# A hybrid decoder trunk: TensorE's instruction order written out for the scan layer, in five bunches a group, and for the last attention head

## The chip, the cores and the metric

One core of one Trainium2 chip runs the whole program once. The metric is device time in microseconds (us), the median of the runs taken. The engines are named as in the profile: PE is TensorE's matmuls and PEld its weight loads, DVE is VectorE, ACT is ScalarE, POOL is GpSimd, SP is the engine that issues most DMAs.

## The reference

The model has four residual layers over a sequence of 512 tokens of width 1024: dilated attention, a gated convolution FFN, a Mamba-2 mixer, and a second FFN, and then a final norm. The change touches the end of the attention, all of the Mamba-2 mixer and the start of the FFN behind it. Shortened:

```python
def ssd_mixer(h, ...):                       # h = rmsnorm(x)
    zxbcdt = h @ w_in                        # 1024 -> z 2048, xs 2048, B 1024, C 1024, dt 32
    xbc = silu(causal_depthwise_conv(xbc, conv_w, conv_b))      # 4 taps
    xs, bm, cm = ...                         # 32 heads of 64; 8 groups of B and C, 128 states
    dt = softplus(dt_raw + dt_bias); a = -exp(a_log)
    y = ssd_chunked_scan(xs, dt, a, bm, cm)  # 4 chunks of 128 tokens:
        # y_diag = ((C B^T) * lmat) (xs dt),  lmat[i,j] = exp(min(cs_i - cs_j, 0)), j <= i
        # states = B^T (decay xs dt), carried over the chunks; y_off = C states * exp(cs)
    y = gated_group_rmsnorm(y + d_skip * xs, z, norm_w, SSM_GROUPS)  # y*silu(z), rms over 256
    return y @ w_out                         # 2048 -> 1024

x = x + dilated_attention_mixer(rmsnorm(x), ...)   # 8 heads, 3 dilations, softmax over the three
x = x + conv_ffn(rmsnorm(x), ...)                  # (silu(gate) * up) @ w_down
x = x + ssd_mixer(rmsnorm(x), ...)
x = x + conv_ffn(rmsnorm(x), ...)
return rmsnorm(x)
```

## The kernel before, in words

Activations lie feature by token, 128 features by 512 tokens in a tile. Each float32 product is made of three float32r products (`mm3`, L129): high part times high part, high times low, low times high. A tile of 128 outputs over 1024 inputs is therefore 24 matmuls of 128x512. The weights are fetched by `load_unit` (L109): a DMA on SP into `raw` (3 buffers), the high part by a cast on ACT (`hi`), the low part by a subtraction on DVE or, for the gate `z`, on POOL (`lo`). `hi` and `lo` have 4 buffers each.

The scan layer works on 8 groups. `project_group` (L639) makes the six products of a group: two of xs, b, c, two of z; on each follow a scaling from PSUM by DVE (`us`, L630), a 4-tap convolution (ACT L510 and three DVE steps L512) and a silu on ACT. `decay_rates` (L576), once at the start, turns the product `wdt` into step sizes by some twenty small DVE steps (`dtw`, then `adt`), sums them by PE (`pa`, `prow`), and writes them to memory as `rows`, from which each head's decay tile `lm` is read back. `scan_group` (L654) is a generator with six steps between its yields: (1) transposes `px`, `pb` and the product `pc`, which make `xdt`, `btok` and `cb`; (2) the decay tiles of two heads, the states `pst`, a second `px`; (3) the outputs `py`, `pf` of the first half, decays and states of the second; (4) the outputs of the second half and `gsq`, the sum of both halves' squares (L762); (5) `ss`, the sum over features by PE, and `rg` on POOL; (6) `prg`, the spreading of `rg` by PE, and the scaled `y`. `write_groups` (L777) makes the output products `wso` from finished `y`, 12 matmuls for two groups.

`weave` runs a generator's steps and puts a share of a list of other work (`fill`) behind each: for group g the six products of group g+1 and the output products of groups long finished. What order the instructions then take on each engine is settled by the tile framework's own scheduler, which may move any instruction past another, except where `tc.manual_schedule` names engines: there these engines keep the order in which the code is written. Before, that holds for PE in `outputs`, in the later part of `last_group`, and at the starts of the FFNs. Once built, the order is fixed: every engine works its list from the front and waits at the first instruction whose inputs are late.

In the attention, head h is worked (`attend`, L347) beside the projections of head h+1: three pairs `qk` (scaled by DVE, rotated by POOL, L321 to L326) and `v`, turned by PE (`pv`). Head 7 has no next head; beside it stand its own `v` and the first parts of the output products `wo` (`wo_first`, L466), which need heads 0 to 6 only; the last head's part (`o7h`, `o7l`) is added at L501.

## Time and profile before

| | us |
|---|---|
| median of 3 runs (1676.91 to 1684.19) | 1677.9 |
| the profiled execution, whole | 1678.81 |
| its span, first to last instruction | 1677.0 |
| PE busy in the span | 1654.9 |
| DVE busy | 1075.1 |
| ACT busy | 693.2 |
| POOL busy | 469.9 |
| PE idle before `wo`, waiting for ACT's `o7h` | 2.1 |
| PE idle before `pf`, waiting for DVE's `prev` | 2.1 |

PE is busy 99% of the span, so all the time in which it does nothing is 22.1 us. The other engines' idle time matters only where PE waits for them. In the rows below, a time in front is that from the span's start; "[2.10 <-ACT o7h L449]" is idle time of the engine and what ended it. Matmuls overlap: a 128x512 product takes 0.38 us from its start to its end, but the next one starts some 0.22 us after it. On DVE, too, one instruction starts a little (some 0.08 us) ahead of the end of the one in front.

### The profile page before, as it was taken

The page shows a single profiled execution, that of the slowest core. Times are in us where ns is not written, and L with a number is a line of the kernel's source. Part 1 is how long each engine was busy: PE and PEld are TensorE (multiplying, and loading weights), DVE is VectorE, ACT ScalarE, POOL GpSimd, SP SyncE. Part 2 cuts the span into 40 slices and gives each one's busy share as a digit, 9 for nine tenths or more (in the row PEclk, how much of TensorE's full clock was granted, in tenths as well). Part 3 has the DMA queues.
Part 4 walks back from the last instruction along what each step waited for, and adds up shares of the span by engine and source line. Part 5 has one row for each costly group of instructions (what it writes and reads, how often), then busy time and mean ns, then how long its engine had stood idle before and what let it go on. Part 6 is the DMA issues. An engine that isn't in the chain of part 4 may idle for free. (4 is left out here: it accounts for less than half of the span.)

```text
span 1677.0 us, 21515 instructions
## 1 busy us (share of the span) xinstructions
PE 1654.9 (99%) x8224; PEld 1401.9 (84%) x8224; DVE 1075.1 (64%) x1794; ACT 693.2 (41%) x1020; POOL 469.9 (28%) x305
## 2 busy tenths in 40 slices
PE   9999999999999999999999999999999999999997
PEld 8888888888888888888888788888888888888887
DVE  5466564366656745745657888787787684574564
ACT  5223332333244423423445665555562542342345
POOL 0443443144413211211232223233222331121124
PEclk9999999999999999999999999999999999999999
DMA  6321222222223323323233222332321232322324
GB/s 218 108 88 64 89 76 88 95 82 76 78 99 126 98 85 107 101 89 113 79 100 132 95 94 95 94 101 101 113 95 56 97 113 88 103 98 89 113 79 135
DMA packets 52343, 165.56 MB, mean 99 GB/s; under 512 B 5841, under 2 KB 8145, under 8 KB 52241
## 3 DMA queue, kind: packets, MB, share of 16 engines
q1 hardware_dynamic: 51152, 163.15, 29.2%
q8 instruction: 65, 1.06, 0.3%
q10 hardware_dynamic: 1088, 1.05, 0.2%
q14 instruction: 38, 0.30, 0.1%
HBM read 162.01 MB, written 2.16 MB: 98 GB/s over the span
## 5 line engine op out<-in xcount | busy, mean ns | idle before, releaser
L127 PE MATMUL u<-xl,hi_u 128*128 128x512 f32 x704 | 270.0, 384 | 1.8 <-DVE xl L176 1.8
L127 PE MATMUL u<-xh,hi_u 128*128 128x512 f32 x704 | 270.3, 384 | 0.0
L127 PE MATMUL u<-xh,lo_u 128*128 128x512 f32 x704 | 269.9, 383 | 0.0
L532 POOL TENSOR_TENSOR au<-au,au 128x512 f32<-128x512 f32 x44 | 57.9, 1316 | 431.9 <-DVE au L512 411.2
L512 DVE SCALAR_TENSOR_TENSOR au<-usu,par,au 128x510 f32<-128x510 f32 (+1 forms) x176 | 162.2, 926 | 6.6 <-ACT au L510 1.7
L325 POOL TENSOR_TENSOR rotqk<-rotqk,sr 32x512 f32<-32x512 f32 x48 | 91.9, 1914 | 257.4 <-DVE rotqk L324 210.0
L118 ACT CAST hi_u<-raw_u 128x1024 fp32r<-128x1024 f32 x88 | 91.1, 1042 | 156.6 <-PE u L127 102.9
L127 PEld LDWEIGHTS u<-xl,hi_u 128*128 128x128 f32 x704 | 131.9, 187 | 27.2 <-DVE xl L176 2.2
L127 PEld LDWEIGHTS u<-xh,lo_u 128*128 128x128 f32 x704 | 131.9, 187 | 25.2
L127 PEld LDWEIGHTS u<-xh,hi_u 128*128 128x128 f32 x704 | 131.9, 187 | 25.2
L127 PE MATMUL qk<-xh,hi_qk 128*128 128x512 f32 x384 | 149.1, 388 | 0.0
L127 PE MATMUL qk<-xl,hi_qk 128*128 128x512 f32 x384 | 148.2, 386 | 0.0
L127 PE MATMUL qk<-xh,lo_qk 128*128 128x512 f32 x384 | 147.1, 383 | 0.0
L527 DVE TENSOR_TENSOR usu<-u,rbc 128x512 f32<-128x512 f32 x88 | 60.5, 690 | 110.6 <-PE u L127 101.3
L119 DVE TENSOR_TENSOR lo_u<-raw_u,hi_u 128x1024 fp32r<-128x1024 f32 x88 | 109.7, 1251 | 24.7 <-ACT hi_u L118 24.7
L545 DVE TENSOR_TENSOR xr<-xr,wd 128x512 f32<-128x512 f32 x40 | 27.2, 686 | 117.1 <-PE wd L127 117.1
L118 ACT CAST hi_qk<-raw_qk 128x1024 fp32r<-128x1024 f32 x48 | 50.2, 1046 | 125.5 <-PE qk L127 73.1
L118 ACT CAST hi_wd<-raw_wd 128x1024 fp32r<-128x1024 f32 (+1 forms) x56 | 52.5, 953 | 118.0 <-PE wd L127 74.8
L321 DVE TENSOR_TENSOR qk<-qk,cr 128x512 f32<-128x512 f32 x48 | 33.0, 687 | 91.0 <-PE qk L127 90.8
L127 PEld LDWEIGHTS qk<-xh,lo_qk 128*128 128x128 f32 x384 | 72.0, 188 | 13.2
L127 PEld LDWEIGHTS qk<-xh,hi_qk 128*128 128x128 f32 x384 | 72.0, 188 | 12.8
L127 PEld LDWEIGHTS qk<-xl,hi_qk 128*128 128x128 f32 x384 | 72.1, 188 | 12.3
(635 smaller groups left out, 3981.1 us busy)
## 6 DMA issues: line engine op xcount, KB each, us to landing
raw_u<-in_wup SPq DMA_DIRECT2D x88, 512.0 KB, 3.2
raw_qk<-in_wqk SPq DMA_DIRECT2D x48, 512.0 KB, 3.2
raw_wd<-in_wdn SPq DMA_DIRECT2D x32, 512.0 KB, 3.2
raw_wd<-in_wdn SPq DMA_DIRECT2D x24, 384.0 KB, 3.0
raw_xs<-in_win SPq DMA_DIRECT2D x16, 512.0 KB, 3.3
raw_z<-in_win SPq DMA_DIRECT2D x16, 512.0 KB, 3.2
lm<-rows SPq DMA_DIRECT2D x32, 256.0 KB, 3.8
raw_wso<-in_wso SPq DMA_DIRECT2D x16, 512.0 KB, 3.3
```

Of the source, the lines that this page charges most:

```text
L118: SC.copy(hi[:, s], raw[:, s])
L119: low.tensor_tensor(lo[:, s], raw[:, s], hi.bitcast(F32)[:, s], op=ALU.subtract)
L127: T.matmul(in_turns(dst), w, in_turns(x), start=first, stop=last)
L321: V.tensor_tensor(at(t), of(p), of(cr), op=ALU.mult)
L325: G.tensor_tensor(rot[R, :], rot[R, :], sr[R, :], op=ALU.mult)
L512: V.scalar_tensor_tensor(dst[:, j:], src[:, : S - j], col(c_w + taps - 1 - j), dst[:, j:], op0=ALU.mult, op1=ALU.add,)
L527: V.tensor_tensor(us, p, rbc, op=ALU.mult)
L532: G.tensor_tensor(ab[1], ab[0], ab[1], op=ALU.mult)
L545: V.tensor_tensor(xr[m], xr[m], p, op=ALU.add)
```

## The change

PE's order is written down for the last head, and for the scan layer from `decay_rates` to the first products of the FFN behind it. A group's six steps become five bunches: `behind` puts step 6 of the group before behind step 1 of this group. `weave` shares the fill by its count of matmuls (`products`) in place of its length. The output products of groups 5 and 6 move from the last loop pass to `last_group`. `hi` and `lo` have 5 buffers. `prg` takes a `side` bank. A fifth `wo_first` (of `wo` 4, in a `side` bank) stands behind the last head's steps, and `wo` 5 to 7 take `mm` banks. In the tail DVE's and ACT's orders are written out as well, with `row` and `low` in place of `prep`.

```diff
-    wh = ctx.enter_context(tc.tile_pool(name="wh", bufs=4))
+    wh = ctx.enter_context(tc.tile_pool(name="wh", bufs=5))
...
     def weave(core, stages, fill):
+        cost = [getattr(f, "products", 24) for f in fill]
         done = 0
         for i in range(stages):
             next(core, None)
-            until = -(-len(fill) * (i + 1) // stages)
-            for f in fill[done:until]:
-                f()
-            done = until
+            while done < len(fill) and sum(cost[:done]) * stages < sum(cost) * (i + 1):
+                fill[done]()
+                done += 1
...
-        p = mm_bank(f"wo{m}") if m < 3 else aux_bank(f"wo{m}")
+        p = mm_bank(f"wo{m}") if m < 3 or m > 4 else (aux_bank, side_bank)[m - 3](f"wo{m}")
...
-        weave(attend(h), DIL + 2, fill)
+        with ExitStack() as last:
+            if h == NH - 1:
+                last.enter_context(tc.manual_schedule(engines={mybir.EngineType.PE}))
+            weave(attend(h), DIL + 2, fill)
+            if h == NH - 1:
+                wo_first(4)
...
-        prg = along_free(rg, "prg")
+        prg = along_free(rg, "prg", side_bank)
...
-    weave(decay_rates(), 3, ahead[0])
+    def groups():
+        weave(decay_rates(), 3, ahead[0])
+        for g in range(NSG - 1):
...
+            scans.append(scan_group(g, tiles[g], ys))
+            weave(behind(scans), 5, fill)
+    def behind(scans):
+        next(scans[-1])
+        if len(scans) > 1:
+            next(scans[-2], None)
+        yield
+        for _ in range(4):
+            next(scans[-1])
+            yield
...
+        def row(m):
+            w7[m]()
+            SC.activation(xh[m], xr[m], AF.Copy, scale=col(C_FFN + KD + m))
+            if m:
+                low(m - 1)
+            square(m, xr[m], ssum_b)
...
+            row(0)
             unit(0)
+            row(1)
             load7(1)
...
+    with tc.manual_schedule(engines={mybir.EngineType.PE}):
+        groups()
+        last_group()
```

In the order rows that follow, a row names line, operation, output<-inputs with their buffer numbers, and size. The first place is PE in the last head, behind the values (`pg`) of head 6. `sc` are scores; `qk_3690` is head 7's last projection, and `v` its value product. Before:

```order
L423 MATMUL pg_3581<-pt,v_3_2561 128x128
L367 MATMUL sc<-qk_3456,qk_3399 128x128
L368 MATMUL sc<-qk_3574,qk_3520 128x128
L367 MATMUL sc<-qk_3456,qk_3399 128x256
L368 MATMUL sc<-qk_3574,qk_3520 128x128
L127 MATMUL v_3725<-xh_82,hi_v_3720 128x4x32x4
```

With the change, at the same place:

```order
L423 MATMUL pg_3581<-pt,v_3_2561 128x128
L367 MATMUL sc<-qk_3456,qk_3399 128x128
L368 MATMUL sc<-qk_3574,qk_3520 128x128
L369 MATMUL sc<-qk_3690,qk_3638 128x128
L367 MATMUL sc<-qk_3456,qk_3399 128x256
L368 MATMUL sc<-qk_3574,qk_3520 128x128
L369 MATMUL sc<-qk_3690,qk_3638 128x128
L127 MATMUL v_3727<-xh_82,hi_v_3722 128x4x32x4
```

The two scores L369 of the third pair stood behind the 24 matmuls of `v` and five of `wo`; now they stand ahead of `v`. The transposes `pv` of `v`, which stood 19 matmuls of `wo` and two scores behind it, now stand right behind `v`.

The second place is PE at the start of the scan layer, where `pa` takes `adt`, the end of the step sizes' chain. Before:

```order
L127 MATMUL xs_7069<-xh_84,lo_xs_7065 128x4x32x4
L127 MATMUL xs_7069<-xh_85,hi_xs_7064 128x4x32x4
L614 MATMUL pa<-adt,tri 128x128
L615 MATMUL pa<-adt,ones 128x128
L622 MATMUL prow<-tri,adt 32x128 x4
L663 MATMUL px<-ident,axs_6844 128x128 x4
```

With the change:

```order
L127 MATMUL xs_6930<-xl_97,hi_xs_6925 128x4x32x4
L127 MATMUL xs_6930<-xh_89,lo_xs_6926 128x4x32x4
L619 MATMUL pa<-adt,tri 128x128
L620 MATMUL pa<-adt,ones 128x128
L627 MATMUL prow<-tri,adt 32x128 x4
L127 MATMUL z_6984<-xh_82,hi_z_6979 128x4x32x4
```

`pa` moves up past two `z` products and ten matmuls of the next group's xs, 58 matmuls in all, and stands right behind group 0's second xs product.

The third place is DVE in the middle groups, around `gsq` (group 3 here; with the change groups 2, 4 and 5 read alike, group 5 with `lo_c`; groups 0 and 1 have no low part there). `usz` scales a finished product `z` from PSUM, `lo_b` is the low part of a weight, `ms` follows `ss`. Before:

```order
L730 TENSOR_TENSOR yt<-yt,ee 128x384
L731 TENSOR_TENSOR yt<-yt,usz_8258 128x512
L698 TENSOR_SCALAR lm<-lm,acs 128x128 x6
L762 TENSOR_TENSOR gsq<-gsq 128x512
L630 TENSOR_TENSOR usxs_8599<-xs_8574,rbc 128x512
```

With the change:

```order
L736 TENSOR_TENSOR yt<-yt,usz_8700 128x512
L703 TENSOR_SCALAR lm<-lm,acs 128x128 x6
L635 TENSOR_TENSOR usz_8657<-z_8632,rbc 128x512
L119 TENSOR_TENSOR lo_b_8807<-raw_b_8805,hi_b_8806 128x1024
L767 TENSOR_TENSOR gsq<-gsq 128x512
L201 TENSOR_SCALAR ms<-ss 128x4
```

The scaling of the first `z` product and a weight's low part now stand ahead of `gsq`; before, `gsq` came ahead of even the xs product's scaling. On PE `ss`, which takes `gsq`, stood inside that `z` product before in groups 3 to 5 (behind both `z` products in groups 0 to 2), with 15 of its 24 matmuls still to come here:

```order
L127 MATMUL z_8636<-xl_92,hi_z_8631 128x4x32x4
L127 MATMUL z_8636<-xh_84,lo_z_8632 128x4x32x4
L196 MATMUL ss<-ones,gsq 128x1 x4
L127 MATMUL z_8636<-xh_85,hi_z_8631 128x4x32x4
L127 MATMUL z_8636<-xl_93,hi_z_8631 128x4x32x4
```

With the change:

```order
L127 MATMUL z_8632<-xl_97,hi_z_8627 128x4x32x4
L127 MATMUL z_8632<-xh_89,lo_z_8628 128x4x32x4
L196 MATMUL ss<-ones,gsq 128x1 x4
L127 MATMUL z_8675<-xh_82,hi_z_8670 128x4x32x4
L127 MATMUL z_8675<-xl_90,hi_z_8670 128x4x32x4
```

`ss` now stands right behind the last matmul of the first `z` product.

More of the change, by code (lines that the diff above doesn't have):

```diff
@@ L793, in step, with timed @@
             V.tensor_tensor(xr[m], xr[m], p, op=ALU.add)
-            if gs[-1] == NSG - 1:
-                prep(m, xr[m], C_FFN + KD, ssum_b)
-        return load, [lambda m=m: step(m) for m in range(KD)]
+        def timed(m):
+            f = lambda: step(m)
+            f.products = 6 * len(gs)
+            return f
+        return load, [timed(m) for m in range(KD)]
     ys = []
@@ new lines, in last_group, with unit, part @@
+        next(scan)
+        w56[4]()
+        w56[5]()
+        next(scan)
+        w56[6]()
+        load7(0)
+        units = []
+        def unit(i):
+            name = f"u1_{i}"
+            units.append((
+                load_unit(A["wup"][44 + i], name), side_bank(name) if i in (1, 2) else mm_bank(name), name
+            ))
+        def part(i, *ks):
+            (hi, lo), t, _ = units[i]
+            for k in ks:
+                mm3(t, hi, lo, k, xh[k], xl[k], k == 0, k == KD - 1)
+        def row(m):
[4 more added lines that the diff above has]
+            square(m, xr[m], ssum_b)
@@ L855, in last_group, with low @@
+        def low(m):
+            V.scalar_tensor_tensor(
+                xl[m], xr[m], col(C_FFN + KD + m), xh[m].bitcast(F32), op0=ALU.mult, op1=ALU.subtract
+            )
+        with tc.manual_schedule(engines={mybir.EngineType.DVE, mybir.EngineType.Activation}):
+            next(scans[-1], None)
+            w56[7]()
+            row(0)
+            unit(0)
+            row(1)
+            load7(1)
+            row(2)
+            row(3)
+            unit(1)
             part(0, 0)
-            w7[3]()
+            row(4)
@@ L857, in last_group @@
             part(0, 1)
-            part(1, 0, 1)
-            w7[4]()
+            part(1, 0)
+            row(5)
+            unit(2)
             part(0, 2)
+            part(1, 1)
+            row(6)
+            part(0, 3)
             part(1, 2)
-            part(2, 0)
-            w7[5]()
-            part(0, 3)
+            part(2, 0, 1)
+            row(7)
+            low(7)
+            part(0, 4)
             part(1, 3)
-            part(2, 1, 2)
-            w7[6]()
-            part(0, 4)
+            part(2, 2)
```

72 lines of the change are left out of this document (22 added, 50 removed).

## The prediction

> **What bounds the kernel now.** I read the page's first part, then PE's waits, then the busy time by stretch. All sums are against the profiled execution: 1678.8 us, span 1677.0; the median of the runs is 0.9 lower.
>
> ```profile
> PE 1654.9 (99%) x8224; PEld 1401.9 (84%) x8224; DVE 1075.1 (64%) x1794; ACT 693.2 (41%) x1020; POOL 469.9 (28%) x305
> ...
> PE pf L721 <- DVE prev L685: 2.1, 1, 2.1
> PE wo L127 <- ACT o7h L449: 2.1, 1, 2.1
> PE ss L196 <- DVE gsq L762: 2.0, 2, 1.4
> PE u L127 <- DVE xl L176: 1.8, 1, 1.8
> PE prg L208 <- POOL rg L202: 1.7, 1, 1.7
> ...
> 480.00:500.00 20.00, 17.80 (x84) 14.68 (x83) 12.56 (x13) 10.66 (x15) 4.09 (x3) 1.00 0.48 160
> 930.00:956.00 26.00, 23.40 (x116) 19.37 (x116) 23.46 (x50) 17.44 (x25) 1.51 (x2) 0.93 0.35 122
> 956.00:1008.00 52.00, 51.04 (x282) 42.93 (x282) 41.33 (x67) 31.98 (x42) 14.33 (x9) 1.00 0.28 92
> 1008.00:1053.00 45.00, 43.31 (x244) 36.30 (x243) 36.39 (x66) 26.34 (x35) 15.06 (x9) 1.00 0.31 106
> 1153.00:1205.00 52.00, 52.00 (x283) 43.87 (x283) 41.12 (x69) 26.78 (x38) 14.54 (x9) 1.00 0.31 102
> 1205.00:1260.00 55.00, 53.61 (x290) 45.02 (x289) 45.09 (x75) 32.54 (x45) 15.00 (x11) 0.97 0.30 100
> 1260.00:1331.00 71.00, 69.18 (x366) 58.72 (x366) 45.47 (x64) 22.86 (x32) 20.09 (x14) 1.00 0.24 82
> ```
>
> A stretch's row gives its length, then busy time of PE, PEld, DVE, ACT, POOL, then the granted clock. PE is the bound nearly everywhere, and the number of matmuls does not change, so the time moves only with PE's idle time and its clock. The middle groups (1153 to 1205) have no idle time at all. What can be won is 2.2 us in the last head (20.00-17.80) and, from 930 on, 2.6, 1.0, 1.7, 1.4 and 1.8. Two waits cost more than they last:
>
> ```profile
> 486.34:489.75 3.41, 3.36 (x14) 2.55 (x14) 1.60 (x2) 2.01 (x3) 0.00 (x0) 1.00 0.93 324
> 934.98:938.39 3.41, 3.41 (x23) 2.80 (x22) 3.20 (x6) 1.38 (x3) 0.00 (x0) 0.50 0.17 36
> 1011.40:1014.81 3.41, 3.41 (x23) 3.16 (x24) 1.65 (x2) 2.80 (x5) 0.00 (x0) 1.00 0.02 5
> 1249.01:1252.42 3.41, 3.41 (x10) 2.66 (x9) 2.73 (x6) 3.40 (x5) 1.01 (x1) 0.50 0.17 43
> 1300.10:1303.51 3.41, 3.41 (x16) 2.93 (x17) 3.28 (x4) 2.85 (x5) 2.69 (x2) 1.00 0.55 209
> ```
>
> These stretches follow the waits for `o7h`, `prev`, `rg`, the longer one for `gsq`, and `xl`. After `prev` (2.1) and `gsq` (1.4) the clock is granted at half for 3.41 us, which loses 1.7 us each; after the others it stays full.
>
> **Removed.** Last head 2.2; `prev` stretch 2.6+1.7; 1.0; 1.7; `gsq` stretch 1.4+1.7. In the tail (1.8) the new `row` order still has PE wait for `lo_u_1`, which stands behind two further xr and xl steps, for some 1 us, so I count 0.8. Sum 13.1. These go because PE has other matmuls there: 21 of `wo` 4 (4.6 us) behind the last values cover `o7h`'s 2.1, 24 to 36 matmuls stand ahead of each later `pf` and `prg`. The fifth weight buffer I cost at nothing: no wait above is for a weight, and a cast on ACT that runs earlier finds ACT 41% busy. The `side` bank for `prg` costs nothing either: its last reader, `yt` behind `py`, is done over 24 matmuls earlier. SP's and POOL's queues keep their steps in much the same order, and each waits for the engines, not they for it, except where a line below says so.
>
> **Added, last head.** Both scores L369 now stand ahead of `v`, and wait for head 7's last projection to be scaled, shuffled and rotated:
>
> ```profile
> 450.87 0.72 DVE L324 STREAM_SHUFFLE rotqk<-qk 32x512 f32<-32x512 f32 x1
> 451.16 0.39 PE L368 MATMUL sc<-qk,qk 128*128 128x128 f32 x2
> 451.66 2.16 POOL L325 TENSOR_TENSOR rotqk<-rotqk,sr 32x512 f32<-32x512 f32 x1 [3.18 <-DVE rotqk L324]
> 453.90 1.26 POOL L326 TENSOR_TENSOR qk<-qk,rotqk 32x512 f32<-32x512 f32 x1
> ...
> L333 DVE TENSOR_TENSOR tv<-v,rbc x8: 691/692/693, 87.8 to 457.6; 128x512 f32<-128x512 f32 x8
> ...
> L502 DVE TENSOR_TENSOR xr<-xr,wo x8: 1154/1170/1190, 490.0 to 511.1; 128x512 f32<-128x512 f32 x8
> ```
>
> PE would be at L369 at 451.4 and its input is there at 453.90+1.26 = 455.2: 3.8 us. Before, `v` covered that; now `v` and all of PE's list behind it are late by as much, and the bounds are narrow (3.5 to 4.0), for nothing in the chain of four steps has changed. `pv` stands right behind `v` and waits for `tv`: 0.69 plus the last matmul's end and the signal, 1.0. Behind the finals, `wo` 5 to 7 take the banks of `wo` 0 to 2, freed by xr steps of 1.17 each, and `lo` of `wo` 5 stands behind three of them: about 1.6 us of waiting where 0.4 was, 1.2 more (bounds 0 and 2). Sum 6.0.
>
> **Added, step sizes.** `pa` waits for `adt`.
>
> ```profile
> 891.13 5.28 PE xs L127 x24
> ...
> 886.26 2.52 DVE L594 SCALAR_TENSOR_TENSOR dtw<-dtw 128x128 f32<-128x128 f32 x1
> ...
> 903.30 0.69 DVE L630 TENSOR_TENSOR usz<-z,rbc 128x512 f32<-128x512 f32 x1
> ...
> 905.88 0.29 DVE L607 SCALAR_TENSOR_TENSOR adt<-dtt,dtw 128x128 f32<-128x128 f32 x1
> ```
>
> PE would be there at 891.13+5.28 = 896.4. Before, `adt` was done at 905.88+0.29 = 906.2, and `pa` stood far behind it. DVE's list with the change has one step `usz` less (0.6 from its start to the next). Its 2.52 step ran beside a POOL subtraction and would take 0.29, as `adt` does, if that subtraction now runs earlier. So `adt` is there at 906.2-0.6-2.2 = 903.4, or at 905.6 if the step stays long: a wait of 7.0 to 9.2. Some low parts in that list need casts on ACT into weight buffers which PE frees only around 891 and 896, so I take 7.5, near the low end. While PE waits here the other engines go on, which is why I count that group's own `pst` and `prev` waits as gone. Everything behind on PE, 48 matmuls of z first, is late by the wait; nothing gives it back, since PE has no other idle time there.
>
> **Added, `ss`.** DVE's rows of a middle group:
>
> ```profile
> 1135.48 0.54 DVE L726 TENSOR_TENSOR ee<-ee,pf 128x384 f32<-128x384 f32 x1
> 1135.95 0.74 DVE L512 SCALAR_TENSOR_TENSOR ac<-usc,par,ac 128x510 f32<-128x510 f32 x1
> 1136.61 0.28 DVE L698 TENSOR_SCALAR lm<-lm,acs 128x128 f32<-128x128 f32 x1
> 1138.72 0.68 DVE L731 TENSOR_TENSOR yt<-yt,usz 128x512 f32<-128x512 f32 x1
> 1139.33 1.26 DVE L698 TENSOR_SCALAR lm<-lm,acs 128x128 f32<-128x128 f32 x6
> 1140.95 0.69 DVE L762 TENSOR_TENSOR gsq<-gsq 128x512 f32<-128x512 f32 x1 [0.36 <-ACT gsq L733]
> 1141.56 0.68 DVE L630 TENSOR_TENSOR usxs<-xs,rbc 128x512 f32<-128x512 f32 x1
> 1148.08 1.22 DVE L119 TENSOR_TENSOR lo_xs<-raw_xs,hi_xs 128x1024 fp32r<-128x1024 f32 x1
> ...
> 1130.45 1.09 PE L715 MATMUL py<-lm,xdt 128*64 128x128 f32 x16
> 1132.26 0.83 PE L721 MATMUL pf<-ac,prev 128*128 128x128 f32 x6
> 1132.63 2.38 POOL L119 TENSOR_TENSOR lo_z<-raw_z,hi_z 128x1024 fp32r<-128x1024 f32 x1 [13.35 <-ACT hi_z L118]
> 1133.31 2.25 DVE L512 SCALAR_TENSOR_TENSOR ac<-usc,par,ac 128x511 f32<-128x511 f32 x1 [0.94 <-ACT ac L510]
> ```
>
> The floor first. `ss` stands right behind the z product, and ahead of `gsq` DVE has `usz`, which needs that product, and `lo_b`: 0.3 for the product's end and the signal, 0.6+1.14+0.69 on DVE: 2.7 us in groups 2 to 5. In 0 and 1, without a low part, 1.5. Now DVE's whole list. From the end of the second xs product PE has `py` 1.1, `pf` 0.7, 12 matmuls of `wso` 2.7 and 24 of `z` 5.3 (the 5.28 row), so `ss` is due after 9.8 us. In that time DVE has, each some 0.08 shorter from start to start than its row: usxs 0.6, three low parts 3.4, three `yt` steps 1.7, `ee` 0.5, three convolution steps 2.0, an xr 0.6 (a two-input step of 512, like usxs), eight `lm` 1.6; with 0.25 for the first signal 10.7. Only then come `usz`, `lo_b` and `gsq`, 2.4: 13.1. That is 3.3 of waiting in each of four groups. Groups 0 and 1 have no `wso` and one low part: due after 7.1, DVE 7.8 and then 1.3, and it enters the stretch some 0.4 late: 2.4 each. Sum 4x3.3+2x2.4 = 18.0; floor 4x2.7+2x1.5 = 13.8. In groups 6 and 7 `gsq` stands ahead of what waits for PE: nothing. A step on DVE beside a POOL subtraction is drawn out (2.25 beside 2.38, against 0.74), so 1.5 more may come in each of the six: ceiling 27.0. I take the walk, 18.0, since it is made of undisturbed rows, as most are.
>
> **Added, the clock.** Eight waits of some 2.4 to 7.5 us are new. Before, two of five between 1.4 and 2.1 were followed by half clock. Longer ones should be followed by it more often; I take six of eight, 6x1.7 = 10.2, between 2/5 of eight (5.4) and all (13.6).
>
> [...]
>
> **Sum.** 6.0+7.5+18.0+10.2 = 41.7, less 13.1: 28.6 us slower, 1707.4 against 1678.8, and 1706.5 for the median.
>
> **The rivals.**
> (1) The order does what it says: each bunch meets ready inputs, and the 13.1 us are won with only the last head's 6.0 lost: 1672. That needs DVE to reach `gsq` and `adt` in time; it decides if `ss` and `pa` together wait under 7.1 us and the clock stays full. For it: 52 us without any wait in the middle groups before. Against it: `usz` ahead of `gsq` in the order, six times.
> [...]
> (3) POOL's subtractions fall beside DVE's chain in each group: 6x1.5 more: 1716.4. For it: the 2.25 row. Against it: five weight buffers let POOL run earlier.
> (4) Waits at their floors, clock at 5.4: 6.0+7.0+13.8+5.4-13.1 = 19.1: 1698.
>
> **How the numbers follow.** My forecast 0.48, (2) 0.18, (3) 0.16, (4) 0.12, (1) 0.06. The range reaches from below (4) to above (3): 1690 to 1718; what lies outside is mostly (1). A change within 0.5% (8 us, about what a measurement of this kernel can tell) would need the floors, no clock loss and more gains than are seen: 0.04, taken from (4) and (1). Faster 0.04, same 0.04, slower 0.92.
>
> **What would show it.** In PE's waits: `sc` for POOL's `qk` near 3.8, `pv` for `tv` near 1, `pa` for `adt` near 7.5, `ss` for `gsq` six times at 2 to 4, and none for `o7h` or `rg`. Granted clock below 1.00 in most groups. The forecast is wrong if `ss` waits once or twice only, if `pa` finds `adt` ready, or if PE's idle time in the span is under 30 us.

## The result: 3.9% slower, and the profile after

The changed kernel takes 1745.6 us (median; 1743.8 to 1746.8), the kernel before 1680.4 beside it: 1.0387 times as long, 95% interval 1.0358 to 1.0416. The forecast was slower, 1706.5, with a range up to 1718; the loss is 65 us and not 29. The profiled execution of the changed kernel took 1743.75 us, its span 1742.0. Two single runs of the experiments below, 1949 us in 10 and 9724 us in 14, were far slower than the others of the same kernel, and the medians leave them out.

The page's busy times, after (that of before stands in the prediction):

```profile
PE 1676.8 (96%) x8224; PEld 1416.2 (81%) x8224; DVE 1074.5 (62%) x1794; ACT 708.8 (41%) x1030; POOL 469.1 (27%) x305
```

The number of PE's matmuls is the same. So the 65.0 us of span fall into two parts: PE's busy time grew by 21.9 (1676.8 less 1654.9), and its idle time by 43.1 (65.2 in place of 22.1). Nearly all of the growth in busy time is the clock's: PE works 49.7 us at half clock, where before it was 8.1. At half a 128x512 matmul follows the last after 0.43 us, at full clock after 0.22, so of the 41.6 us more at half some 20 are lost, an estimate from these rows. What PE waited for, after; the columns are total us, times, longest:

```profile
PE ss L196 <- DVE gsq L767: 29.9, 7, 5.3
PE pa L619 <- issue: 8.2, 1, 8.2
PE pf L726 <- DVE prev L690: 3.9, 4, 1.3
PE sc L369 <- POOL qk L326: 3.6, 1, 3.6
PE wso L127 <- DVE xr L798: 3.0, 1, 3.0
...
PE u L127 <- DVE xr L798: 0.9, 1, 0.9
PE pv L336 <- DVE tv L333: 0.8, 1, 0.8
...
PE wo L127 <- ACT pt L412: 0.7, 1, 0.7
```

The waits for `o7h` and `rg` are gone, as forecast, and each new wait stands where the order put it. `ss` waits seven times, not six. The page puts `pa`'s wait down to "issue", but it is for `adt`: that step on DVE ends at 911.97, and `pa` starts at 912.07. The busy times by stretch, after (length, PE, PEld, DVE, ACT, POOL, then the granted clock):

```profile
1130.14:1134.73 4.59, 0.00 (x2) 0.00 (x1) 4.54 (x11) 4.55 (x6) 0.00 (x0) 1.00 0.38 130
1135.36:1138.77 3.41, 3.41 (x11) 2.83 (x12) 0.16 (x1) 1.92 (x3) 1.01 (x1) 0.50 0.35 133
1188.57:1193.88 5.31, 0.00 (x0) 0.00 (x0) 5.26 (x12) 5.18 (x6) 0.00 (x0) 0.95 0.50 163
1193.38:1200.21 6.83, 6.33 (x19) 5.36 (x20) 0.61 (x2) 3.04 (x4) 1.01 (x1) 0.50 0.23 79
1144.00:1203.00 59.00, 53.68 (x273) 44.94 (x272) 40.49 (x68) 28.43 (x38) 14.27 (x9) 0.94 0.27 90
```

The middle groups, which had no idle time at all before, lose 4.6 to 5.3 us in a group (here 59.00 less 53.68). The first and third rows are waits of `ss`: PE does nothing, DVE and ACT are busy from end to end. Behind each the clock is at half for one stretch of 3.41 us or two.

### The profile page after: what moved, and what is told of

The parts are those of the page before. It is cut to its first block, busy times and chain, and to the rows that moved or that the text cites. A ratio compares the mean times of both kernels' runs of the same rounds, so it can differ in the third digit from the quotient of the medians.

```text
span 1742.0 us, 21510 instructions
## 1 busy us (share of the span) xinstructions
PE 1676.8 (96%) x8224; PEld 1416.2 (81%) x8224; DVE 1074.5 (62%) x1794; ACT 708.8 (41%) x1030; POOL 469.1 (27%) x305
## 3 DMA queue, kind: packets, MB, share of 16 engines
q1 hardware_dynamic: 51152, 163.15, 27.9%
q10 hardware_dynamic: 1088, 1.05, 0.2%
## 4 chain that ended last, share of the span: by engine, by line
PE 85%; DVE 8%; ACT 3%; issue 3%; DMA 1%; POOL 1%; POOLq 0%; SPq 0%; ACTq 0%; DVEq 0%
PE u L127 27%; PE qk L127 15%; PE wd L127 12%; PE v L127 7%; PE z L127 4%; PE wso L127 3%; PE xs L127 3%; PE b L127 2%; PE c L127 2%; PE wo L127 2%; PE wz L127 1%; DVE axs L517 1%; DVE ac L517 1%; PE ss L196 1%; PE pp L410 1%
## 5 line engine op out<-in xcount | busy, mean ns | idle before, releaser
L127 PEld LDWEIGHTS qk<-xh,hi_qk 128*128 128x128 f32 x384 | 72.1, 188 | 12.8
```

The source lines that it names most:

```text
L127: T.matmul(in_turns(dst), w, in_turns(x), start=first, stop=last)
```

## The experiments

Each was run beside the kernel before on the same chip; the ratio is to that kernel, with its 95% interval. "Less" and "more" are medians against the changed kernel's 1745.6; medians of different batches can differ by some 3 us, as those of the kernel before did (1678.5 to 1681.6), so a gain or loss of that size is not told from nothing.

**1. `ss` later** (1.0186, 1.0164 to 1.0208).

```diff
-    def behind(scans):
+    def behind(scans, steps=3):
+        if len(scans) > 1:
+            next(scans[-2])
         next(scans[-1])
```

> The changed kernel, with one step moved: the sum `ss` over features stands on PE behind the second z product of its group and not behind the first (24 matmuls, some 5.3 us, later). In the changed kernel's profile `ss` waits 29.9 us in seven places. Theory A (the chain on DVE that ends in `gsq` reaches its end 3 to 5.3 us too late for the place in which `ss` stands, and each wait then costs the clock one or two stretches of 3.41 us at half): all seven waits go, PE's idle time falls by 27 to 30 us, and of the 51 us at half clock behind those waits at least 30 go, which gives back 15 to 25 us more: 1690 to 1703. Theory B (PE runs ahead of DVE for the whole group, so that a wait which goes from `ss` comes back at the next product that takes something from DVE, `px` or `prg`): idle time stays within 8 us of the changed kernel's 65, time 1735 to 1746.

The two added lines put the step with `ss` of the group before ahead of this group's transposes. Measured: 1711.3, 34.4 less. PE's waits and its busy time in groups 1 to 5:

```profile
PE pa L619 <- issue: 8.2, 1, 8.2
PE pc L751 <- DVE ms L201: 5.2, 1, 5.2
PE prg L208 <- POOL rg L202: 5.2, 1, 5.2
```

```profile
1011.00:1270.00 259.00, 259.00 (x1414) 219.63 (x1413) 214.82 (x358) 152.72 (x202) 69.42 (x44) 1.00 0.30 101
```

Between 1011 and 1270 PE does not rest once and the clock stays full. So the place of `ss` carried those waits, and PE does not outrun DVE over a whole group. Where a group has little work to put between, at the first and the last, the wait came back in another place, 5.2 us each; that is why the gain in idle time was 18 us (65.2 to 47.1) and not 27 to 30, and the time lies above theory A's range.

**2. Without `gsq` on DVE** (1.0304, 1.0276 to 1.0332).

```diff
-        V.tensor_tensor(sq0, sq0, sq1, op=ALU.add)
...
-        inv_rms(sq0, 2 * P, rg)
+        inv_rms(sq0, 2 * P, rg, sq1)
```

> The changed kernel, with DVE's addition `gsq` dropped: `ss` stays where it stands and sums the two squares itself with twice as many small matmuls, so it waits for ACT's second square and not for DVE's sum. The theory that DVE's `usz` and `lo_b` ahead of `gsq` are the end of the chain: the second square is made at 1132.28 in group 3 where `gsq` ends at 1134.7, so each `ss` wait becomes some 1.7 to 2.3 us shorter, 12 to 16 us of idle time in all, 3 to 5 us of added PE work for the small matmuls, and some of the half clock goes too: 10 to 25 us less, 1721 to 1736. Rival (the chain up to the last square, ACT's casts with it, carries the wait, and DVE's last steps only follow from it): under 5 us of idle time goes, 1740 to 1748.

Measured: 1729.9, 15.7 less. The group of `ss` matmuls (instructions, busy us and mean ns, idle us before them), with this edit:

```profile
L196 PE MATMUL ss<-ones,gsq 128*128 128x1 f32 x128 | 19.1, 271 | 11.8 <-ACT gsq L738 11.8
```

The waits fell from 29.9 to 11.8, for 6.3 us more of small matmuls (19.1 in place of 12.8). DVE's last steps (`usz`, `lo_b`, `gsq`) are thus 18 us of the waits, 2.6 in a group; but the second square itself is 0.8 to 2.4 us late in every one. Both theories had a part: the time is theory A's.

**3. The wait half filled** (1.0384, 1.0367 to 1.0402).

```diff
         p = aux_bank("ss")
+        for _ in range(keep):        # 12
+            long_product(p, xh[0][:, 0:P], xh[1], True, True)
```

> The changed kernel, with twelve matmuls of 128x512 that serve nothing put on PE ahead of each `ss` (their result is overwritten). They take 2.7 us each time and stand where PE waits 2.9 to 5.3 us; in the last group `ss` does not wait, so there they add 2.7 us. This takes the clock by itself. Theory A (a wait of 3 to 5 us costs one or two stretches of 3.41 us at half clock, a shorter one often none): the waits shrink to 0.2 to 2.6 us with everything else in its place, the half clock behind `ss` falls from 51 us to under 25, and the time falls by 10 to 20 us less the 2.7: 1728 to 1738. Theory B (the clock closes for what `ss` itself is, a row of matmuls with one column, or for another reason than the rest): half clock stays near 51 us and the time is the changed kernel's plus 0 to 5: 1744 to 1751.

Measured: 1744.0, 1.6 less, so no clear change: the lower edge of theory B's time. (The 51 us in the expectation also counted the stretches behind the scores and in the tail; behind `ss` it is 41.0.) The waits shrank to 1.3 to 1.9 us, and the half clock behind them fell, but only to 23.9 us (granted clock 0.97 from 960 to 1310, where the changed kernel has 0.94): rests this short, with the row of `ss` behind them, were still followed by half. Experiment 8 shows what part that row has; experiment 15 fills the whole wait.

**4. `pa` later** (1.0376, 1.0353 to 1.0399).

```diff
-        weave(decay_rates(), 3, ahead[0])
+        ...                          # both z products of group 0, then pa, prow
```

> The changed kernel, with `pa` and `prow` moved on PE behind the two z products of group 0 (48 matmuls, 10.6 us later); the z products fill the time in which PE waited 8.2 us for `adt`. Theory A (`pa` alone paid): the 8.2 us go, and with them the half clock of 10.24 us that began at 906.66, worth 5.1: 11 to 14 us less, 1731 to 1735. Theory B (what hangs on `pa`, the decay tiles read back from memory through `rows`, is late by the same 10 us, and group 0 waits for them in turn at `py` or `pf`): under 5 us gained, 1740 to 1750.

Measured: 1743.5, 2.1 less, so no clear gain. Theory B holds. PE's waits:

```profile
PE pf L726 <- DVE prev L690: 5.6, 2, 4.3
```

`pa` no longer waits, but `prev`, which is made from what `pa` gives, is 4.3 us late at `pf`, and `pb` waits 1.2 for ACT. Idle time falls by 3.2 us in all, and PE's busy time rises by 4.6, with 82.6 us at half clock in place of 72.7 (granted clock 0.977 and 0.980). The chain behind `pa` sets the start of the scan, not the place of `pa` alone.

**5. The scan's order left to the scheduler** (1.0139, 1.0122 to 1.0156).

```diff
-    with tc.manual_schedule(engines={mybir.EngineType.PE}):
-        groups()
+    groups()
+    with tc.manual_schedule(engines={mybir.EngineType.PE}):
         last_group()
```

> The changed kernel, with the order on PE no longer written down for the scan layer up to its last group; the five bunches, the sharing of the fill, the buffers, the head and the tail stay as changed. The order is then the scheduler's, and in it `ss` stands behind both z products and 16 matmuls of the next xs, and `pa` 61 matmuls further back. Theory A (the written order itself puts `ss` and `pa` where their inputs are late): the 29.9 us of `ss` and the 8.2 of `pa` go, at most 6 us come back in other waits; the half clock in the middle falls from 61 us to under 21; what stays over the kernel before is the head (5 to 8) and the tail (4 to 7): 1688 to 1700. Theory B (the five bunches as such make DVE late, whoever orders PE): over 15 us of waits for DVE stay in the scan, 1715 to 1740.

Measured: 1705.2, 40.4 less, the largest share of the loss. What PE waits for then:

```profile
PE pst L681 <- POOL xdd L671: 6.0, 2, 4.1
PE pc L751 <- DVE ms L201: 5.2, 1, 5.2
PE ss L196 <- DVE gsq L767: 4.5, 3, 2.2
```

Theory A holds for what went (29.9 to 4.5 at `ss`, all of `pa`); that at most 6 us come back was wrong: `pst` and `pc` wait 11.2. `pst` stands in groups 0 and 1, where no order is written down in this run. `pc` (at 1271) is in the last group, whose order this edit leaves written down.

**6. The last head's order left to the scheduler** (1.0354, 1.0338 to 1.0369): the line that enters `manual_schedule` is taken out.

> The changed kernel, with the order on PE no longer written down for the last head; the fifth first part of `wo` stays. In the scheduler's order the two scores of the third pair stand behind `v` and five matmuls of `wo`, and the last values have no `wo` work behind them. Theory A (the head's terms were read rightly): the waits of 3.6 (scores) and 0.8 (`pv`) go with the 3.41 us at half clock behind them, 2.1 for `o7h` come back: 3 to 5 us less, 1740.5 to 1743. Theory B (the loss lies behind the head, in the banks that `wo` 5 to 7 take): under 1.5 us, 1744 to 1747.

Measured: 1741.2, 4.4 less. In the last head PE now has only one wait over 0.2 us:

```profile
PE wo L127 <- ACT o7h L449: 2.1, 1, 2.1
```

Theory A.

**7. The old tail** (1.0357, 1.0342 to 1.0373): the last group's rows, squares and splits in the order of before.

> The changed kernel with the tail as it was (the last group's output products with each row's square and split in the old order; DVE's and ACT's orders there not written out). In the changed kernel PE waits there 0.9, 3.0, 0.5 and 0.4 us, with 6.83 us at half clock from 1360.6 on. Theory A (the new rows put steps of one row ahead of what frees a bank for the next): these waits go, 1.8 come back, and the half clock goes: 5 to 7 us less, 1738.5 to 1741. Theory B (the tail is late because the group ahead of it is late): the same waits come up under other names, 1744 to 1747.

Measured: 1741.9, 3.7 less. PE's waits in the tail, with this edit:

```profile
PE u L127 <- DVE xl L176: 3.0, 2, 1.8
```

The changed kernel's 3.0, 0.9 and 0.4, beside which its clock was at half for 6.83 us from 1360.64 on, are gone; 3.0 came back and not 1.8, so the gain is below theory A's, and theory B falls.

**8. A ladder of waits, for the clock.**

```diff
+            T.transpose(q[:, 0:P], ident, ident)
+            SC.copy(s, q[:, 0:P])
+            for _ in range(n):               # 0 to 14, by the product
+                G.tensor_tensor(s, s, ident, op=ALU.mult)
+            T.transpose(q[:, P : 2 * P], s, ident)
```

> The kernel before, with fourteen waits of graded length set into PE's work in the first FFN, where it has none: in the middle of a product PE makes one transpose, ACT copies it, POOL multiplies the copy 0 to 14 times, and PE takes the result in a second transpose before it goes on with its 128x512 products. PE's order in this FFN is written down so that nothing fills the wait. The time will be longer by the waits, some 0.7 to 8 us each, and says nothing; what is read is the granted clock behind each wait. Theory A (the clock is set for one stretch of 3.41 us by how much of the stretch before PE rested, wherever that stretch happens to begin): waits under 1 us never close it, waits of 1.4 to 2.5 sometimes, 3 to 4.5 always for one stretch and at times for two, over 5 always for at least two. [...]

Wait in us and half clock behind it, from the rows of the second transposes and the record of the granted clock: 0.36 and 1.40 none; 2.25 one stretch of 3.41; 3.35 none; 3.85, 4.00, 4.36, 4.62, 5.96 and 6.54 two (6.83); 6.58, 8.19, 8.72 and 9.25 three (10.24). The two that decide are 2.25, which was followed by half clock, and 3.35, which was not:

```profile
556.76 0.33 PE L159 MATMUL ladu<-ident,su 128*128 128x128 f32 x1 [2.25 <-POOL su L158]
...
760.08 0.33 PE L159 MATMUL ladu<-ident,su 128*128 128x128 f32 x1 [3.35 <-POOL su L158]
```

The stretches of 3.41 us in which they lie, and one behind a longer wait:

```profile
553.60:557.01 3.41, 1.17 (x7) 0.75 (x6) 2.68 (x3) 1.02 (x3) 3.02 (x3) 1.00 0.49 154
557.01:560.42 3.41, 3.41 (x10) 2.64 (x9) 0.00 (x0) 0.10 (x1) 0.00 (x0) 0.50 0.02 5
754.98:758.40 3.42, 1.75 (x9) 1.18 (x7) 2.53 (x3) 0.85 (x2) 1.21 (x3) 1.00 0.34 115
758.40:761.81 3.41, 1.73 (x8) 1.48 (x9) 0.00 (x0) 0.62 (x1) 2.90 (x3) 1.00 0.10 38
...
601.38:604.79 3.41, 2.57 (x7) 2.10 (x8) 0.00 (x0) 0.00 (x0) 0.70 (x2) 0.50 0.00 0
604.79:608.21 3.42, 3.42 (x10) 2.65 (x9) 0.36 (x1) 0.78 (x1) 0.00 (x0) 0.50 0.00 0
```

The stretches lie on one grid: in the changed kernel's trace the spells at half begin at 456.11, 906.66, 968.10, 1015.89 and so on to 1360.64, each a whole number of stretches of 3.413 us behind the one before. The wait of 2.25 lies within one stretch, which has 1.17 of PE's work in it: the next stretch is at half. The wait of 3.35 falls across the border of two, with 1.75 and 1.73 of work in them: both are at full clock. The stretch at 601.38 is at half, PE rested 0.84 in it (3.41 less 2.57), and the next one is at half again. In these rows, then, the clock followed PE's work in a fixed stretch, not the length of the wait: theory A's mechanism, though not its "3 to 4.5 always".

One kind of work does not fit into that count: the rows of `ss`, eight matmuls of 128x1. Two stretches of the kernel before show it, the first behind the wait for `o7h`, the second behind the longer one for `gsq`:

```profile
484.42:487.83 3.41, 1.49 (x7) 1.30 (x8) 1.38 (x2) 1.20 (x3) 0.00 (x0) 1.00 0.77 233
1245.59:1249.01 3.42, 2.03 (x14) 1.87 (x14) 3.37 (x8) 3.40 (x6) 0.00 (x0) 1.00 0.38 145
```

The first has less work, 1.49, and the next stretch was at full clock; the second has 2.03 and was followed by half. In its 2.03, `ss` takes 1.05, and other matmuls run for 1.11. If only the time of other matmuls than 128x1 is counted, the stretches of the traces of before and after, behind the first 20 us, fall in order. At full clock, those with up to 1.29 us of work were followed by half, those with 1.49 or more by full; at half, those with up to 1.62 were followed by another at half (2.57 in this run), those with 2.80 or more by full. With the 128x1 rows counted, a stretch at full clock with 2.31 us was followed by half (1729.29 in the changed kernel). The figures are from the rows, whose ends are modelled.

**9. ACT without table loads** (1.0336, 1.0319 to 1.0353).

```diff
-                SC.activation(e_[half, P:512], t[half, P:512], AF.Exp)
+                SC.activation(e_[half, P:512], t[half, P:512], AF.Square)
...
-                SC.activation(t, t, AF.Exp)
+                SC.activation(t, t, AF.Square)
```

> The changed kernel with the two exponentials of the decay tiles (`lm`, `ee`) replaced by squares, which need no other table on ACT; the output is then another, the time of each instruction is not. 44 table loads of 1.28 us go from ACT's list, and the order of all else on every engine is the same. In group 3 of the changed kernel DVE waited 1.57 us for the cast `hi_xs`, which stood on ACT behind such a load, and its walk up to `gsq`, 13.1 us as forecast, became 14.7. Theory A (ACT's list is what the forecast's walk left out): the `ss` waits fall by 1.3 to 1.6 us in each of groups 0 to 5, from 29.9 to 20 or 22 us in all, with 3 to 7 us of half clock: 1729 to 1738. Theory B (DVE's own list is the whole of it; a cast that comes earlier finds DVE busy): the `ss` waits stay within 2 us of 29.9, 1743 to 1748.

Measured: 1737.3, 8.3 less, which is theory A's time; the `ss` waits are 24.7, between the two theories. In groups 0 and 1 they fell from 4.0 to 2.3 each, in group 6 from 2.9 to 0.3, as theory A has it. In groups 2 to 5 they stayed (4.9 to 5.0). What DVE waits for in groups 2 to 5, first in the changed kernel:

```profile
DVE lo_xs L119 <- ACT hi_xs L118: 7.7, 8, 2.3
...
DVE lm L703 <- DMA lm<-rows: 0.8, 1, 0.8
```

Then with the table loads gone:

```profile
DVE lm L703 <- DMA lm<-rows: 6.3, 8, 1.2
```

One late input took the place of the other: where the cast no longer holds DVE up, the decay tile's read-back does, 6.3 us for 7.7.

**10. Three parts undone together** (1.0091, 1.0076 to 1.0107): 5, 6 and 7 in one.

> The changed kernel with three parts undone together: no written order on PE in the last head, none in the scan layer up to its last group, and the old tail. What stays is the five bunches, the fill shared by matmuls, the moved output products, `prg`'s bank and the fifth buffer. Theory A (the parts add up): alone they gave 4.4, 40.4 and 3.7 us, so 1745.6-48.5 = 1697, 1694 to 1700; the 16 us that stay over the kernel before lie in the bunches, above all in the wait of 5.2 us at `pc` of the last group and the half clock behind it. Theory B (the parts overlap: much of what one loses another hides): 1684 to 1693 or over 1702.

Measured: 1695.4, 50.2 less; alone they gave 48.5. The parts add up. 16 us over the kernel before stay, with PE's waits

```profile
PE pst L681 <- POOL xdd L671: 5.7, 2, 3.9
PE pc L751 <- DVE ms L201: 5.2, 1, 5.2
```

and 12.1 us more idle time than before (34.3). That the bunches cost this under any order is not shown: `pc` stands in the last group, whose order is still written down, and `pst` waits 3.2 at the same place with the fifth buffer alone (run 11).

**11. The fifth buffer alone**, in the kernel before (1.0004, 0.9995 to 1.0013).

> The kernel before with the fifth buffer for `hi` and `lo` alone. Theory A (no wait of the kernel before is for a weight, so a buffer more moves only work off the path): within 4 us of it. Theory B (casts that run earlier put ACT and POOL ahead into DVE's chain): 5 us slower or more, with new waits for `gsq` or `prev`.

Measured: 1680.9 beside 1679.3. It costs and gains nothing in time, as the forecast had it, though waits change places: PE waits 3.2 at `pst`, and no longer for `o7h` and `gsq`.

**12. A first corrected order** (1.0278, 1.0259 to 1.0298): `ss` behind `pc`, `prg` two products later, the scan's start the scheduler's, `v` ahead of the last head's scores, the old tail.

> A written order with the places put right: `ss` stands behind the next group's `pc`, `prg` two products behind that, group 6's `ss` behind the first z product of group 7 and `prg` behind the second; the start of the scan layer with its first group is left to the scheduler; in the last head `v` stands ahead of the scores and the fifth part of `wo` behind the last values; the tail is the old one. Theory A (what the written order lost, it lost in a few places, and elsewhere it is better than the scheduler's): no wait for `gsq`, `rg` or `o7h`; of the 22 us of PE's idle time before, 7 to 9 go, and one of two stretches of half clock: 1668 to 1675 where the kernel before has 1680. Theory B (the start of the scan or the last groups, which have little work to put between, wait in new places): 1680 to 1695.

Measured: 1725.5. Theory B, and above its range. PE's waits:

```profile
PE ss L196 <- DVE xdt L685: 11.5, 5, 3.4
PE pf L741 <- DVE prev L705: 7.3, 3, 5.4
PE wso L127 <- ACT y10h L791: 4.4, 1, 4.4
```

`ss` now waits for a bank that `xdt` on DVE has to free, `wso` for a `y` that came later with `prg`, and `pf` of the last group for `prev`, which has only two output products left ahead of it. In the last head, though, only 0.7 us of waiting is left.

**13 and 14. Seven buffers for the decay tiles**, without table loads (1.0319, 1.0304 to 1.0335) and alone (1.0398, 1.0370 to 1.0427).

```diff
-                t = t2("lm", "lm", 5, lp)
+                t = t2("lm", "lm", 7, lp)
```

> The changed kernel with squares in place of the decay tiles' exponentials (as in the run with that edit alone; the output is another, the time of each instruction is not) and with seven buffers for the decay tiles `lm` in place of five, so that their read-back from memory need not wait for the outputs that use the old ones. Theory A (the cast on ACT and the read-back are the whole of what the forecast's walk of DVE left out): the `ss` waits in groups 2 to 5 fall from 4.9 to the walk's 3.3, those in groups 0 and 1 stay at 2.3: some 18 us in all, 1726 to 1733. Theory B (DVE finds a third late input, or its list is longer than walked): waits of 4.5 to 5 in groups 2 to 5, 1734 to 1740.

> The changed kernel with seven buffers for the decay tiles `lm` in place of five, and nothing else. Theory A (in the changed kernel the cast `hi_xs` ends DVE's wait, and the read-back hides behind it): the `ss` waits stay within 2 us of 29.9, 1742 to 1748. Theory B (the read-back is late for itself, and ACT's exponentials with it): 4 us or more of the `ss` waits go, 1732 to 1741.

Measured: 1733.1 and 1744.8; the `ss` waits 23.7 and 29.9. Alone, theory A: nothing. Together, the time is at theory A's edge, 4.2 us less than run 9, but that is the clock's (57.8 us at half in place of 71.9, granted clock 0.984 and 0.980); idle time did not fall (59.7 after 58.8), and 4.6 to 4.9 of waiting stay in groups 2 to 5, as theory B has it. DVE still waits 5.7 us there for `lm` from `rows`: the transfers are still issued right behind `py` (51.1 us of SP's waits there are for it). The two buffers gave no slack.

**15. The wait filled** (1.0337, 1.0322 to 1.0352): as 3, with 20 matmuls.

> The changed kernel with twenty matmuls of 128x512 that serve nothing ahead of each `ss` (4.5 us, their result is overwritten). They fill nearly all of each wait (2.9 to 5.3 us) and add some 7 us in all: 4.5 in the last group, which has no wait, 1.6 in group 6, 0.5 in each of groups 0 and 1. The rest of the program is late by the same as in the changed kernel, so that what the time falls by, with these 7 added, is the clock alone. Theory A (the half clock behind `ss`, six stretches of 3.41 or 6.83 us, 41 us in all, costs half its length, and ends when PE does not rest): under 5 us of it stay, 1745.6-20.5+7 = 1732, 1728 to 1737. Theory B (it costs less, since part of it lies on time in which PE waits in any case): 1739 to 1748.

Measured: 1735.7, 10.0 less. PE in groups 0 to 6, in the changed kernel:

```profile
960.00:1310.00 350.00, 318.42 (x1652) 267.51 (x1651) 246.45 (x425) 182.91 (x242) 86.96 (x55) 0.94 0.26 86
```

With the twenty matmuls:

```profile
960.00:1310.00 350.00, 346.74 (x1872) 293.18 (x1871) 259.84 (x439) 190.84 (x251) 93.28 (x60) 1.00 0.27 89
```

The 160 added matmuls are 35.7 us of work (0.223 each); the waits of 29.9 went. PE's busy time rose by 19.9 (1696.7 in all), so the clock gave back 35.7-19.9 = 15.8 us. That is the price of the half clock behind `ss` by itself: 15.8 for 41.0 us at half. The pace says the same: PE worked in 35.8 of the 41.0 us, which at half loses some 17, less 1.2 for a second stretch behind the scores in this run. The granted clock is 1.00 from 960 to 1310 here, so the row of `ss` alone was not followed by half either. Theory A, near its upper end.

**16. A second corrected order** (1.0105, 1.0090 to 1.0120): `ss` and `prg` as in 1, group 0's `prg` later, the last group in another order, head and start as in 12.

> A second written order: `ss` stands behind the second z product and ahead of the next group's transposes, with `prg` behind these, as in the run in which groups 1 to 5 had no wait; `prg` of group 0 two products later; the last group with its first z product ahead of its states, then group 6's `ss`, the second z product and `prg`. The start with group 0 is the scheduler's, the last head has `v` ahead of the scores and the fifth part of `wo` behind the last values (no wait for scores, `pv` or `o7h` in the run before), and the tail is the old one. Theory A (the written order loses only where a place is wrong): in PE's waits 2 to 4 us at the start of the scan, 3 in the tail, nothing over 1 between; idle time 17 to 21 where before it was 22.1, one or two stretches of half clock: 1674 to 1681, not to be told from the kernel before or a little faster. Theory B (each place moved makes another late): new waits over 2 us in the last groups or the middle ones, 1683 to 1700.

Measured: 1697.0, 48.7 less, and still 18 us over the kernel before. PE's waits, and its busy time in the middle:

```profile
PE pst L696 <- POOL xdd L686: 5.5, 2, 4.2
PE ss L196 <- DVE gsq L782: 4.7, 1, 4.7
PE px L683 <- ACT axs L656: 2.9, 1, 2.9
```

```profile
1010.00:1240.00 230.00, 230.00 (x1261) 195.30 (x1261) 191.76 (x306) 130.22 (x173) 68.44 (x43) 1.00 0.31 101
```

In the middle the written order is as good as the scheduler's and no better: no idle time in 230 us with 1261 matmuls, where the kernel before has none from 1012 to 1240 either, 228 us with 1264 (its 1.4 at `ss` comes later, at 1247, in group 6). At the scan's start (`pst`, and group 0's `ss`) and in the last group (`px`) theory B holds. No version of these experiments is faster than the kernel before.

**17 and 18. A tile of its own for the read-back**, without table loads (1.0431, 1.0416 to 1.0447), and with `gsq` off DVE as well (1.0298, 1.0281 to 1.0316).

```diff
-                dma(t, rows[h : h + 1, :].to_broadcast([P, S]))
+                row = t2("row", "row", 2, lp)
+                dma(row, rows[h : h + 1, :].to_broadcast([P, S]))
```

> The changed kernel with squares in place of the decay tiles' exponentials (the output is another, the time of each instruction is not), and with the rows read back from memory landing in tiles of their own, two of them, from which DVE's subtraction writes `lm`; the transfer then waits for DVE's step on an older row and no longer for the outputs `py`. PE's order is the same, and between the second xs product and `gsq` DVE has the same steps. Theory A (the cast on ACT and the read-back are the whole of what the forecast's walk of DVE left out): no wait of DVE over 0.3 us in the stretch ahead of `gsq`; the `ss` waits in groups 2 to 5 fall from 4.9 to the walk's 3.3, 2.3 stay in groups 0 and 1: 17 to 19 us in all, 1725 to 1733. Theory B (a third late input): 4.5 to 5 us in groups 2 to 5, 1733 to 1740.

> As the run before, with DVE's addition `gsq` dropped as well and both squares summed by `ss` itself. The last steps of DVE ahead of `ss` were `usz`, `lo_b` and `gsq`, 2.4 us in groups 2 to 5 and 1.3 in groups 0 and 1; without them `ss` waits for ACT's second square. Theory A (the causes add up: cast, read-back, and DVE's last steps): 0.5 to 1.2 us in each of groups 2 to 5, under 0.9 in groups 0 and 1, some 5 us in all, and less than 14 us of half clock behind `ss`: 1710 to 1720. Theory B (with these gone the next late input shows): 10 us or more in all, 1720 to 1730.

Measured: 1751.5 and 1730.0; the `ss` waits 34.8 and 11.8. Both theories A fall, and run 17 lies above its theory B as well (run 18's holds): DVE waited more for the read-back, not less. Run 17, groups 2 to 5:

```profile
DVE lm L704 <- DMA row<-rows: 9.8, 8, 1.8
```

With two tiles for the rows, each transfer waits until the row two before it has been read: SP waits 23.2 us there for ACT's step `ee`, eight times. So the read-back could not be taken out of DVE's list by these edits. That it holds DVE up once the cast is out of the way is seen in the rows of 9, 13 and 17; what the `ss` waits in groups 2 to 5 would be without both stays open.

## Why the prediction was wrong, step by step

The sum in the span, forecast and measured, less the waits of before at the same place (in brackets, new less old). The measured parts add up to 63.8 of the 65.0 us, the forecast to 28.6; of the 35.2 between, the clock is 15.1, `ss` 12.3 and the rest 7.8:

| | forecast | measured |
|---|---|---|
| last head (6.0-2.2; 3.6+0.8+1.7-2.1) | +3.8 | +4.0 |
| `pa` | +7.5 | +8.2 |
| `ss` (18.0-2.4; 29.9-2.0) | +15.6 | +27.9 |
| scan's start, `prg` (`pst`, `pf`, `rg`) | -4.3 | -0.7 |
| tail | -0.8 | +2.5 |
| clock (10.2-3.4; PE's busy time) | +6.8 | +21.9 |

**Right:** the direction, the places, and the small terms. The scores wait 3.6 (3.8 was forecast), `pv` 0.8 (1.0), the `wo` finals and first parts 1.7 where the forecast had 0.4 and 1.2 more; run 6 gave it back. `pa` waits 8.2, within 7.0 to 9.2. The fifth buffer costs nothing (run 11).

**The `ss` term, 18.0 against 29.9.** The walk followed DVE's list and counted its steps, and left out that DVE itself waits in it. Group 3 after, DVE:

```profile
1120.25 0.69 DVE L635 TENSOR_TENSOR usxs<-xs,rbc 128x512 f32<-128x512 f32 x1 [0.91 <-PE xs L127]
1122.51 1.23 DVE L119 TENSOR_TENSOR lo_xs<-raw_xs,hi_xs 128x1024 fp32r<-128x1024 f32 x1 [1.57 <-ACT hi_xs L118]
...
1132.26 0.68 DVE L635 TENSOR_TENSOR usz<-z,rbc 128x512 f32<-128x512 f32 x1
1132.86 1.21 DVE L119 TENSOR_TENSOR lo_b<-raw_b,hi_b 128x1024 fp32r<-128x1024 f32 x1
1133.99 0.68 DVE L767 TENSOR_TENSOR gsq<-gsq 128x512 f32<-128x512 f32 x1
```

And ACT, which it waits for:

```profile
1118.46 0.62 ACT L738 ACTIVATE gsq<-yt 128x512 f32<-128x512 f32 x1
1119.09 1.28 ACT L707 ACT_TABLE_LOAD   x1
1120.39 1.15 ACT L707 ACTIVATE lm<-lm 128x512 f32<-128x512 f32 x2
1121.44 1.03 ACT L118 CAST hi_xs<-raw_xs 128x1024 fp32r<-128x1024 f32 x1
```

The xs product ends at 1120.2; PE reaches `ss` 9.9 us later (9.8 forecast), and `gsq` ends 14.5 us later (13.1 forecast). The 1.57 us behind the cast make up the difference: 4.6 of waiting in place of 3.3. In groups 0 and 1 it is the same 1.6 or so (4.0 for 2.4): DVE waits 0.25 for a cast and 1.28 for ACT's convolution step `axs`, and run 9 took this away by ACT's table loads alone. In group 6, set at nothing, DVE waited 1.91 for a cast on ACT and 0.78 for the second square, 2.7 of the 2.9. In groups 2 to 5 the cast is one of two late inputs at about the same time, the read-back the other (9, 13, 17); how the 5.9 us that were missed there divide between them stays open. The step that failed is thus "I take the walk, 18.0, since it is made of undisturbed rows": undisturbed steps do not make an undisturbed list. POOL, which rival (3) and the ceiling named, was not the reason: in groups 0 to 5 it runs no subtraction from the end of the xs product to `gsq`.

**The clock term, 10.2 against about 25** (21.9 more than before, where the two old stretches, 3.4, went as forecast). "I take six of eight, 6x1.7 = 10.2" was wrong twice. The clock closed in ten places (seven `ss`, `pa`, the scores, the tail), and in seven of them for two stretches or three: of these, each but the last had 1.62 us of work or less in it (`ss` left out), and the last 2.80 or more (run 8). The waits of before that the term was sized on are 1.4 to 2.1 long and cost one stretch at most. Which of them were followed by half was no matter of chance, two in five, nor of their length: the stretches with 1.3 us of work (`prev`) and 1.1 (`gsq`, with `ss` left out) were followed by half, those with 1.5 (`o7h`), 1.6 (`xl`) and 2.1 (`rg`) were not. Run 15 measured the part behind `ss`: 15.8 us.

**The scan's start and the tail, together 6.9 us off.** "I count that group's own `pst` and `prev` waits as gone" failed: `pf` waits 3.9 us in four places, probably since `prev` hangs on the same late chain as `pa`: in run 4, with `pa` later, it waits 5.6. In the tail the forecast named `lo_u_1` alone; what waits is `wso`, 3.0, for the bank that an xr step frees (run 7).

None of the rivals came near.

## What to carry to other kernels

When an order is written down for one engine, walk the list of the engine it waits for with that engine's own waits in it, casts, table loads and transfers included: here the walk without them gave 18 us, and the trace 30. A wait put where there had been none cost the clock here as well, about half as much again (15.8 for 29.9), and shortening it to 1.3 to 1.9 us brought back less than half of the time at half clock (41.0 to 23.9 us). And where each moved step has little other work to stand behind, at the first and last pass of a loop, moving it only moves the wait: two other orders (1 and 16) had no wait in the middle and waits of up to 5.2 us at the ends.

## What the hardware showed that was not expected

The border of the clock's stretches decided more than a wait's length: in run 8 a rest of 3.35 us that fell across it left the clock full, one of 2.25 inside a stretch was followed by half. To come back to full took more work: in the traces of before and after, stretches of 3.41 at full clock with 1.49 us of work or more were followed by full, but one at half with 2.57 was followed by another at half (run 8), and in the changed kernel waits of 2.9 to 5.3 us went with 6.83 us at half in six of ten places. And a row of 128x1 matmuls did not count as work: the 2.03 us in the stretch before 1249.01, 1.05 of them such a row, did not keep the clock full.
